# One core's hybrid decoder layer: queries and keys of both head pairs ahead of the other projections, the second norm's roots after the fourth product of the MLP, and MLP operands of two tile groups made during the output projection

## The chip, the cores and the metric

The kernel runs on one core of one Trainium2 chip. The metric is the device time of one execution in microseconds (us), as the median of several runs. An execution of this kernel runs five engines side by side: TensorE (PE, with its weight loads shown as PEld), VectorE (DVE), ScalarE (ACT), GpSimd (POOL), and SyncE (SP), which issues the loads and stores. Each engine takes its instructions in the order in which the program lists them, and waits at one until its operands and its target are free. So the order of the list on each engine is the schedule.

## The reference

One decoder layer over 1024 tokens of width 1024; the MLP's inner width is 4096. All data are float32.

```
u = rms_norm(x, norm1_g)
z = u @ w_in                       # 3584 columns
cb, cc, ch = split(z[:, :1536]);  rq, rk, rv, rg = split(z[:, 1536:], 4)
y_conv = group_rms_norm(cb * causal_dwconv3(cc * ch, conv_w), conv_norm_g, 8)
q = rotary(rq);  k = rotary(rk) * 128**-0.5          # 4 heads of 128
o = chunkwise_retention(q, k, rv)                    # chunks of 128 tokens
#   per chunk: o = (q k^T * decay) v + (q * xi) S;   S = gamma^128 S + (k * zeta)^T v
y_ret = group_rms_norm(o, ret_norm_g, 4) * silu(rg)
x = x + concat([y_conv, y_ret]) @ w_out
u = rms_norm(x, norm2_g)
x = x + (relu(u @ w_up) ** 2) @ w_down
out = rms_norm(x, final_norm_g)
```

## The kernel before

**Data.** Activations lie transposed: a tile is 128 features by 1024 tokens, cut in two halves of 512 tokens (`hs`). Every float32 operand is split into a high and a low part (`uh` and `ul`, `wh` and `wl`, the two halves of a `U` tile), and one product is three matmuls: high by high, high by low, low by high. ACT writes the high part, DVE or POOL subtracts to get the low part. `prepare` does this for the weight pieces some products ahead, from a planned list (`plan`, `parts`).

**Stages.** First come the values `v` of the retention heads and the token sums of the first norm (`rtok`, one root per token). Then the columns of `w_in`, 128 at a time, in the order of `IN_FIRST`: `rot_tiles` makes a rotated query or key of two heads from two column tiles (numbers 12 to 19), and `whole` makes a conv or gate tile (numbers 0 to 7). `tile_in` runs one column tile in four quarters, each with 12 matmuls of 128x512, into two PSUM banks. The remaining columns go by pairs (`pair_in`) and are computed by seven products in place of eight on combined operands, which `rights` prepares. Then comes `w_out` (`group`, four groups of eight steps, each step 12 matmuls), and then the MLP's up and down projections in blocks of seven products (`product`, `down_product`). The first block of the MLP is written by hand as a list, `rest`, with one entry for each of its 14 products (7 products for 2 tile pairs, `EARLY`). `at` counts them from 0.

**Rotary.** The first column tile's evacuation is four DVE multiplications into `ac` and `as`. The second's is eight DVE and four POOL operations, which give `q` (and the same for `k`).

**The first norm.** `spread_norms` copies the roots along a row (a DVE copy to a `t` tile) and multiplies by the identity matrix (`spread`, L304, 16 matmuls in all), so that ACT can write the root of each token to all partitions (`R`, `R2`). Conv and gate tiles are scaled by `R`; q and k are not, since the retention applies the norm per chunk. In the kernel before, it stands between q and k of pair 0.

**Retention.** `retention(p, q, k)` is a generator with one step for each of eight chunks and two more to drain. A step issues the scores of a chunk (L542, L547), the products of the chunk before (L571 to L579), and the transposes of the one before that (L609). DVE masks the scores to `h` and updates the state `S`; ACT and DVE make the output's root `m`, and ACT writes the normalized `h`.

**What sets the order.** A small planner runs while the program is written. It keeps a modelled clock per engine (`clock`, `now`). Work that isn't written in line is a task (`Task`, `spawn`), and `tick`, called after each quarter of a tile or each product, lets the tasks that are due issue their next instructions. A task yields the name of a mark that it waits for (`yield "retention", 1`). What has been issued is final. `force` runs a task up to a mark.

**The second norm.** `out_evac` adds each `w_out` result to the residual `x2` and collects squares in `sums_`. `token_rnorms` (L286) adds these over the partitions by 16 matmuls with one column each, takes root and reciprocal and copies them along rows; `spread` makes `r_half`. The MLP block's `take` adds products up; a finished block of 128x512 goes through `put`, which applies `max(c, 0) * r` and a square. The residual tiles that aren't needed for a while are written to DRAM (`put_aside`, pool `kept`) and read back (`fetch_back`).

**MLP operands.** `U` holds them by name: `11`, `21`, `22` are scaled quarters of the tiles, `t1` to `t4` sums of them; `put_hi` or `put_scaled_hi` is ACT's part, `put_lo` or `put_scaled_lo` DVE's. `group_todo(j)` lists those that are made during `w_out`, by step counted from the group's start; the others are made in `rest`. `new_basis` changes the residual tiles to the basis of the down products, on POOL.

All ACT, DVE and POOL operations are recorded through one helper, so their line in the profile is L65. L365 is the matmul of `mm`, L1173 that of the down products, L323 that of the values. These are the lines that a sentence can't say as well:

```
IN_WHOLE = [[0, 1, 2], [3, 4, 5, 6, 7]]
IN_FIRST = [12, 13, 16, 17] + IN_WHOLE[0] + [14, 15, 18, 19] + IN_WHOLE[1]
MLP_ORDER = (1, 2, 6, 5, 3, 7, 4)
EARLY = 2
```

## Time and profile before

| | us |
|---|---|
| median of 3 runs | 1115.47 (1114.19 to 1116.75) |
| profiled execution, own time | 1113.53 |
| its span | 1111.7 |
| PE busy | 1064.8, 96% of the span |
| DVE busy | 872.1, 78% |
| ACT busy | 462.1, 42% |
| POOL busy | 542.7, 49% |
| mean granted clock of TensorE | 0.985 of full speed |

The span is what the profiler saw of the program; the execution's own time is 1.83 us longer. Busy time is the sum over an engine's instructions. Matmuls are pipelined, so that a matmul's duration is longer than the distance to the next one. In the lists of instructions, a name is the program's with its number left out: `b` is a PSUM bank, `t` a temporary tile, `r` a raw weight piece or a row of roots.

### The profile page before, as it was taken

What the parts mean: (1) busy time and instruction counts of PE and PEld (TensorE: products, weight loads), DVE (VectorE), ACT (ScalarE), POOL (GpSimd) and SP (SyncE); (2) the same over time, 40 slices, a digit from 0 to 9 for tenths busy, and PEclk for the clock granted to TensorE, in tenths of its full rate; (3) what the DMA queues carried; (4) which work ended last, traced back from release to release, by engine and by line L of the source; (5) the groups of instructions that cost most, each with busy time, mean ns of one, the idle gap of its engine ahead of it and who ended that gap; (6) DMA issues with size and microseconds to landing.
All of it is one profiled execution on the core that took longest, in us unless ns stands there. A gap on an engine that the chain in (4) does not pass through costs nothing.

```text
span 1111.7 us, 13918 instructions
## 1 busy us (share of the span) xinstructions
PE 1064.8 (96%) x4916; PEld 885.2 (80%) x4916; DVE 872.1 (78%) x1207; ACT 462.1 (42%) x909; POOL 542.7 (49%) x377
## 2 busy tenths in 40 slices
PE   7979999999998699979999999999999999999997
PEld 6858888887777588868888888888888888888886
DVE  8441547548999745579999989989989899899945
ACT  8211461367336434344344333433343343434453
POOL 6130323414667323535827629538257276284553
PEclk9989999999999899989999999999999999999998
DMA  7111101240121523022130130121211211200204
GB/s 266 60 57 29 39 29 48 86 142 10 39 57 48 198 80 121 8 88 84 48 89 26 49 94 29 55 69 38 76 39 53 90 28 49 85 20 19 67 10 152
DMA packets 38294, 74.40 MB, mean 67 GB/s; under 512 B 4305, under 2 KB 6481, under 8 KB 38225
## 3 DMA queue, kind: packets, MB, share of 16 engines
q1 hardware_dynamic: 38224, 73.51, 21.0%
q8 instruction: 39, 0.64, 0.2%
q14 instruction: 31, 0.25, 0.1%
HBM read 67.73 MB, written 5.77 MB: 66 GB/s over the span
## 4 chain that ended last, share of the span: by engine, by line
PE 75%; DVE 12%; issue 2%; ACT 2%; POOL 1%; DVEq 0%; POOLq 0%; ACTq 0%
PE b L365 49%; PE b L1173 22%; DVE wl L65 2%; DVE z L65 2%; DVE r L65 1%; DVE U L65 1%; DVE x L65 1%; DVE t L65 1%; PE b L571 1%; PE b L542 1%; PE b L573 1%; PE b L579 1%; DVE xs L65 1%; DVE cv L65 1%; PE b L304 1%
## 5 line engine op out<-in xcount | busy, mean ns | idle before, releaser
L65 ACT CAST wh<-r 128x512 fp32r<-128x512 f32 x286 | 177.0, 621 | 375.4 <-PE b L365 195.7
L65 DVE TENSOR_TENSOR wl<-r,wh 128x512 fp32r<-128x512 f32 x249 | 227.5, 916 | 112.2 <-ACT wh L65 111.4
L365 PE MATMUL b<-U,wh 128*128 128x512 f32 x992 | 308.6, 392 | 7.1 <-DVE t L65 4.2
L65 POOL TENSOR_TENSOR r<-r,r 128x512 f32<-128x512 f32 x136 | 207.9, 1531 | 131.2 <-DVE wl L65 79.5
L1173 PE MATMUL b<-V,wh 128*128 128x512 f32 x784 | 241.9, 389 | 0.4 <-POOL V L65 0.4
L365 PEld LDWEIGHTS b<-U,wh 128*128 128x128 f32 x992 | 187.3, 189 | 47.8 <-issue 5.8
L65 DVE TENSOR_TENSOR x<-x,b 128x512 f32<-128x512 f32 (+1 forms) x320 | 197.9, 663 | 29.9 <-PE b L365 29.9
L365 PE MATMUL b<-U,wl 128*128 128x512 f32 x496 | 194.0, 391 | 0.0
L1173 PEld LDWEIGHTS b<-V,wh 128*128 128x128 f32 x784 | 147.1, 188 | 31.7 <-POOL V L65 0.8
L65 POOL TENSOR_TENSOR t<-t,t 128x512 f32<-128x512 f32 x70 | 106.7, 1529 | 102.6 <-ACT t L65 56.6
L1173 PE MATMUL b<-V,wl 128*128 128x512 f32 x392 | 152.5, 389 | 0.0
L65 POOL TENSOR_TENSOR wl<-r,wh 128x512 fp32r<-128x512 f32 x37 | 49.8, 1350 | 166.4 <-ACT wh L65 150.3
L365 PEld LDWEIGHTS b<-U,wl 128*128 128x128 f32 x496 | 93.8, 189 | 19.8
L365 PE MATMUL b<-uh,wh 128*128 128x512 f32 x320 | 106.5, 398 | 2.3 <-DVE z L65 2.3
L365 PE MATMUL b<-ul,wh 128*128 128x512 f32 x320 | 104.9, 393 | 1.6 <-DVE ul L65 1.5
L365 PE MATMUL b<-uh,wl 128*128 128x512 f32 x320 | 104.4, 391 | 0.0
L1173 PEld LDWEIGHTS b<-V,wl 128*128 128x128 f32 x392 | 73.6, 188 | 15.3
L65 POOL TENSOR_TENSOR V<-t,V 128x512 fp32r<-128x512 f32 x35 | 49.1, 1404 | 67.2 <-ACT V L65 67.2
L65 DVE TENSOR_TENSOR t<-t,b 128x512 f32<-128x512 f32 x112 | 75.8, 677 | 1.7 <-POOL t L65 1.2
L65 ACT ACTIVATE t<-t 128x512 f32<-128x512 f32 x64 | 40.3, 631 | 79.4 <-DVE t L65 78.7
L365 PEld LDWEIGHTS b<-ul,wh 128*128 128x128 f32 x320 | 60.3, 189 | 15.7 <-DVE ul L65 2.9
L365 PEld LDWEIGHTS b<-uh,wl 128*128 128x128 f32 x320 | 60.3, 189 | 12.9
(153 smaller groups left out, 1442.7 us busy)
## 6 DMA issues: line engine op xcount, KB each, us to landing
r<-w_up_t SPq DMA_DIRECT2D x64, 256.0 KB, 2.6
r<-w_down_t SPq DMA_DIRECT2D x56, 256.0 KB, 2.6
r<-w_in_t SPq DMA_DIRECT2D x48, 256.0 KB, 2.6
xt<-xT SPq DMA_DIRECT2D x16, 256.0 KB, 5.4
xs<-xT SPq DMA_DIRECT2D x8, 512.0 KB, 6.1
r<-w_out_t SPq DMA_DIRECT2D x16, 256.0 KB, 2.6
x<-xT SPq DMA_DIRECT2D x8, 512.0 KB, 7.9
outT<-out SPq DMA_DIRECT2D x6, 512.0 KB, 2.9
```

What stands on the lines that cost most here:

```text
L65: return f(out, *args, **kw)
L304: nc.tensor.matmul(b[:, c * P : (c + 1) * P], d, ident, start=True, stop=True)
L365: nc.tensor.matmul(b, a[:, k, :], rhs(n, k)[r], start=(start and i == 0), stop=(stop and i == len(ops) - 1),)
L542: nc.tensor.matmul(bs[:, js[j]], k[j][:, sl], q[j][:, sl], start=True, stop=True)
L571: nc.tensor.matmul(bo[:, js[j]], sc[:, js[j]], vj[j], start=True, stop=(S is None))
L573: nc.tensor.matmul(bo[:, js[j]], q[j][:, psl], S[:, js[j]], start=False, stop=True)
L579: nc.tensor.matmul(bk[:, js[j]], kz[:, js[j]], vj[j], start=True, stop=True)
L1173: nc.tensor.matmul(b, a, r, start=(i == 0), stop=(i == len(ops) - 1))
```

## The change

It has three parts.

1. `IN_FIRST` and the main loop take the query and key tiles of both head pairs first and the whole tiles after them. `spread_norms` is cut in two: `norm_rows` copies the roots along one row of 128x1024 after pair 0's queries, and the matmuls and ACT's writes follow after pair 1's keys. `retention(0)` therefore runs while pair 1's rotary tiles are computed and `retention(1)` while the first whole tiles are. Each has its own task entry, and the second waits for the end of the first.
2. `token_rnorms` is cut in `token_roots` (matmuls, root) and `rnorms` (reciprocal, row copies). In the MLP's first block the matmuls go from after the second product (`at == 1`) to after the fourth, the reciprocals to after the sixth, and `spread` from after the fourth product to after the ninth. Results are taken at once; a `put` that comes before the roots is kept in `waiting`.
3. For the tile groups 0 and 1 the operands `t3`, `t2`, `22` and `t4` are all made during `w_out`, and two more residual tiles are put aside, so that `rest` only has those of groups 2 and 3.

The diff:

```diff
 IN_PAIRS = [(8, 9), (10, 11), (20, 21), (22, 23)]
-IN_FIRST = [12, 13, 16, 17] + IN_WHOLE[0] + [14, 15, 18, 19] + IN_WHOLE[1]
+IN_FIRST = [12, 13, 16, 17, 14, 15, 18, 19] + IN_WHOLE[0] + IN_WHOLE[1]
 SLOT, LOOK, PE_MARGIN, LATE = 2.57, 2.0, 1.2, 0.0
...
 
-    def token_rnorms(sums_, r, pool_=None):
+    def token_roots(sums_, r, pool_=None):
 
...
         act.activation(r, b[:, :n], AF.Sqrt, bias=eps, scale=1.0 / D)
+        return r
+
+    def rnorms(r):
+
+        n = r.shape[-1]
         dve.reciprocal(r, r)
...
 
+    def token_rnorms(sums_, r, pool_=None):
+        return rnorms(token_roots(sums_, r, pool_))
+
     def spread(wide, pool_=None):
...
 
-    def spread_norms():
+    def norm_rows():
+        d = unit(s="d").rearrange("p (a b) -> p a b", b=P)
+        dve.tensor_copy(d, rtok[:, :, None].to_broadcast([P, NC_, P]))
+        return d
+
+    def spread_norms(d):
 
         for half, sl in enumerate(hs):
-            r = rtok[:, 4 * half : 4 * half + 4]
-            d = tmp().rearrange("p (a b) -> p a b", b=P)
-            dve.tensor_copy(d, r[:, :, None].to_broadcast([P, 4, P]))
-            b = spread([d[:, j] for j in range(4)])
+            b = spread([d[:, 4 * half + j] for j in range(4)])
             act.copy(R[:, sl], b)
...
 
-    o_n, retention_task = {}, [None]
+    o_n, retention_task = {}, [None, None]
 
...
         js = [slice(j * P, (j + 1) * P) for j in range(2)]
+        if p:
+            yield "retention", 0
         for c in range(NC_ + 2):
...
                         mark(("o", h0 + j, pc // 4), act)
-            retention_task[0].ready = max(clock[act], clock[dve])
+            retention_task[p].ready = max(clock[act], clock[dve])
             if c == NC_:
...
         if p == 0:
-            spread_norms()
+            rows_ = norm_rows()
         k = rot_tiles(*ropes)
...
         spawn(retention(p, q, k), max(clock[dve], clock[pool]))
-        retention_task[0] = procs[-1]
+        retention_task[p] = procs[-1]
         del q, k
-        if p == 0:
-            for f in IN_WHOLE[0]:
-                whole(f)
+    spread_norms(rows_)
+    for f in IN_WHOLE[0]:
+        whole(f)
 
...
     ct = ctx.enter_context(tc.tile_pool(name="ct", bufs=11))
-    kept = ctx.enter_context(tc.tile_pool(name="kept", bufs=3, space=bass.MemoryType.DRAM))
+    kept = ctx.enter_context(tc.tile_pool(name="kept", bufs=5, space=bass.MemoryType.DRAM))
     rv = ctx.enter_context(tc.tile_pool(name="rv", bufs=8))
...
 
-        t1 = lambda: un[j][:, lo_]
-        t3 = lambda: un[j][:, hi_]
-        return {
+        hi_of = lambda *names: [lambda x=x: put_hi(x, j, source(x, j)) for x in names]
+        lo_of = lambda *names: [lambda x=x: put_lo(x, j, source(x, j)) for x in names]
+        todo = {
             2: [lambda: put_scaled_hi("11", j, j, 0)],
...
             5: [lambda: put_scaled_lo("21", j, 4 + j, 0)],
-            8: [lambda: sum1(j), lambda: put_hi("t1", j, t1())],
-            9: [lambda: put_lo("t1", j, t1()), lambda: sum3(j)],
-            10: [lambda: sum2(j)] + [lambda: put_hi("t3", j, t3())] * (j < 3),
-            11: [lambda: put_lo("t3", j, t3())] * (j < 3),
+            8: [lambda: sum1(j)] + hi_of("t1"),
+            9: lo_of("t1") + [lambda: sum3(j)],
+            10: [lambda: sum2(j)],
         }
+        if j < 2:
+            todo[10] += hi_of("t3")
+            todo[11] = lo_of("t3") + hi_of("t2")
+            todo[12] = lo_of("t2") + [lambda: put_scaled_hi("22", j, 4 + j, 1)]
+            todo[13] = [lambda: put_scaled_lo("22", j, 4 + j, 1), lambda: sum4(j)] + hi_of("t4")
+            todo[14] = lo_of("t4")
+            todo[15] = [lambda: put_aside(4 + j)]
+        return todo
 
...
     todo[24] += [lambda: put_aside(2)]
-    todo[30] = [lambda: put_hi("t2", 0, source("t2", 0)), lambda: put_hi("t2", 1, source("t2", 1))]
+    todo[30] = [lambda: put_hi("t2", 2, source("t2", 2)), lambda: put_scaled_hi("22", 2, 6, 1)]
     for j in range(4):
...
 
-    r_half = [None, None]
+    r_half, waiting = [None, None], []
 
...
         def put(self, name, c):
-            self.c[name] = c
             r = r_half[int(name[1]) - 1]
+            if r is None:
+                waiting.append(lambda: self.put(name, c))
+                return
+            self.c[name] = c
             dve.scalar_tensor_tensor(c, c, 0.0, r, ALU.max, ALU.mult)
...
     rest = [
-        todo[32] + lo("t2", dve, 0, 1) + hi("t2", 2) + call(hi22, 0, 1),
-        todo[33] + lo("t2", dve, 2) + todo[34] + hi("t2", 3) + call(lo22, 0, 1) + call(hi22, 2, 3),
-        lo("t2", dve, 3) + hi("t3", 3) + call(lo22, 2, 3),
-        call(sum4, 0, 1) + hi("t4", 0, 1) + lo("t3", dve, 3),
-        call(sum4, 2, 3) + hi("t4", 2, 3) + call(fetch_back, 0, 1, 2),
-        lo("t4", dve, 0, 1),
+        todo[32] + lo("t2", dve, 2) + hi("t3", 2),
+        todo[33] + call(lo22, 2) + todo[34] + call(hi22, 3) + hi("t2", 3),
+        call(sum4, 2) + lo("t2", dve, 3) + hi("t3", 3) + lo("t3", dve, 2),
+        call(sum4, 3) + call(lo22, 3) + hi("t4", 2, 3) + call(fetch_back, 0, 1),
+        lo("t3", dve, 3) + call(fetch_back, 2, 4, 5),
         lo("t4", dve, 2),
         lo("t4", dve, 3),
-        call(new_basis, 5),
         call(new_basis, 7),
+        call(new_basis, 5),
         call(new_basis, 3),
         [],
+        [],
         [lambda: v_split(early, 1, 0)],
...
         b = early[p].product(n)
-        if at == 1:
-            wides = [token_rnorms([sums_[h]], rtok[:, 4 * h : 4 * h + 4]) for h in range(2)]
+        if at == 0:
             up.fetch(4)
-        if at == 3:
-            r_half[:] = [spread(w, pn) for w in wides]
         prepare()
...
         put_now()
-        if at == 2:
-            b2 = b
-            continue
-        if at == 3:
-            early[0].take(n, b2)
         early[p].take(n, b)
+        if at == 3:
+            roots = [token_roots([sums_[h]], rtok[:, 4 * h : 4 * h + 4]) for h in range(2)]
+        if at == 5:
+            wides = [rnorms(r) for r in roots]
+        if at == 8:
+            r_half[:] = [spread(w, pn) for w in wides]
+        while r_half[0] is not None and waiting:
+            waiting.pop(0)()
 
```

The order of the instructions shows it at three places. In these rows the first number is the place in the engine's list, then come the line, the operation, output and inputs with their numbers, the shape, and how many of it follow each other.

On PE, between pair 0's queries and its keys, before. The first two rows end the queries' second tile (weights `wl_531`), the last two begin the keys' first tile (`wh_564`):

```order
286 L365 MATMUL b_604<-ul_157,wh_530 128x512
287 L365 MATMUL b_605<-ul_157,wh_530 128x512
288 L365 MATMUL b_604<-uh_149,wl_531 128x512
289 L365 MATMUL b_605<-uh_149,wl_531 128x512
290 L304 MATMUL b_684<-ident,t_682 128x128 x4
291 L304 MATMUL b_693<-ident,t_691 128x128 x4
292 L365 MATMUL b_702<-uh_142,wh_564 128x512
293 L365 MATMUL b_703<-uh_142,wh_564 128x512
```

The same place after:

```order
286 L375 MATMUL b_604<-ul_157,wh_530 128x512
287 L375 MATMUL b_605<-ul_157,wh_530 128x512
288 L375 MATMUL b_604<-uh_149,wl_531 128x512
289 L375 MATMUL b_605<-uh_149,wl_531 128x512
290 L375 MATMUL b_686<-uh_142,wh_564 128x512
291 L375 MATMUL b_687<-uh_142,wh_564 128x512
292 L375 MATMUL b_686<-ul_150,wh_564 128x512
```

The spread's matmuls have left this place. After the change they stand on PE between pair 1's keys (weights `wl_1106`) and the first whole tile (`wh_1190`), with the row tile `d_682`:

```order
648 L375 MATMUL b_1314<-ul_157,wh_1105 128x512
649 L375 MATMUL b_1315<-ul_157,wh_1105 128x512
650 L375 MATMUL b_1314<-uh_149,wl_1106 128x512
651 L375 MATMUL b_1315<-uh_149,wl_1106 128x512
652 L312 MATMUL b_1399<-ident,d_682 128x128 x4
653 L312 MATMUL b_1406<-ident,d_682 128x128 x4
654 L375 MATMUL b_1413<-uh_142,wh_1190 128x512
655 L375 MATMUL b_1414<-uh_142,wh_1190 128x512
```

So some 360 rows of PE's list lie between the queries' end and the spread. On DVE, the evacuation of pair 1's second query tile (banks `b_1417`, `b_1418`) before:

```order
128 L65 TENSOR_TENSOR wl_1477<-r_1362,wh_1476 128x512
129 L65 TENSOR_TENSOR t_1480<-b_1417,rope_277 128x512
130 L65 TENSOR_TENSOR t_1481<-b_1417,rope_276 128x512
131 L65 TENSOR_TENSOR q_1416<-ac_1332,t_1480 64x512
132 L65 TENSOR_TENSOR q_1415<-t_1481,as_1333 64x512
133 L65 TENSOR_TENSOR t_1488<-b_1418,rope_277 128x512
134 L65 TENSOR_TENSOR t_1489<-b_1418,rope_276 128x512
135 L65 TENSOR_TENSOR q_1416<-ac_1332,t_1488 64x512
136 L65 TENSOR_TENSOR q_1415<-t_1489,as_1333 64x512
137 L65 TENSOR_TENSOR wl_1527<-r_1405,wh_1526 128x512
138 L65 TENSOR_TENSOR ac_1496<-b_1498,rope_276 128x512
```

and after (banks `b_942`, `b_943`; `bk` and `causal` mark the retention's masks, `S` its state, `m` its roots):

```order
98 L65 TENSOR_TENSOR t_1109<-b_942,rope_277 128x512
99 L65 TENSOR_TENSOR t_1110<-b_942,rope_276 128x512
100 L65 TENSOR_TENSOR q_941<-ac_834,t_1109 64x512
101 L65 TENSOR_TENSOR q_940<-t_1110,as_835 64x512
102 L65 TENSOR_TENSOR t_1117<-b_943,rope_277 128x512
103 L65 TENSOR_TENSOR t_1118<-b_943,rope_276 128x512
104 L65 TENSOR_TENSOR q_941<-ac_834,t_1117 64x512
105 L65 TENSOR_TENSOR q_940<-t_1118,as_835 64x512
106 L65 SCALAR_TENSOR_TENSOR h_1130<-b_1125,bk,causal 128x128 x2
107 L65 SCALAR_TENSOR_TENSOR S_1143<-S_1074,b_1136 128x128 x2
108 L65 SCALAR_TENSOR_TENSOR m_1147<-m_1147,bq 128x2
109 L65 RECIPROCAL m_1147<-m_1147 128x2
```

The same eight operations now have operations of pair 0's retention ahead of them and behind them, and before the change they had none.

On DVE, in the first products of the MLP's first block (`U` are operands; `un` holds their sums; `sm` the norm's weights; `wl` low parts of weights), before:

```order
377 L65 TENSOR_TENSOR U_3771<-un_3623,U_3771 128x512
378 L65 SCALAR_TENSOR_TENSOR un_3623<-x_3066,sm,un_3623 128x512
379 L65 TENSOR_TENSOR U_3775<-un_3459,U_3775 128x512
380 L65 SCALAR_TENSOR_TENSOR un_3623<-x_3066,sm,un_3623 128x512
381 L65 SCALAR_TENSOR_TENSOR U_3777<-x_3063,sm,U_3777 128x512
382 L65 SCALAR_TENSOR_TENSOR U_3779<-x_3064,sm,U_3779 128x512
383 L65 TENSOR_TENSOR wl_3856<-r_3317,wh_3855 128x512
384 L65 TENSOR_TENSOR U_3832<-un_3623,U_3832 128x512
385 L65 SCALAR_TENSOR_TENSOR U_3836<-x_3065,sm,U_3836 128x512
386 L65 SCALAR_TENSOR_TENSOR U_3838<-x_3066,sm,U_3838 128x512
387 L65 TENSOR_TENSOR wl_3889<-r_3489,wh_3888 128x512
388 L65 SCALAR_TENSOR_TENSOR un_3132<-x_3063,sm,un_3132 128x512
```

and after:

```order
376 L65 TENSOR_TENSOR un_3645<-un_3645 128x512
377 L65 TENSOR_TENSOR U_3743<-un_3469,U_3743 128x512
378 L65 TENSOR_TENSOR wl_3819<-r_3495,wh_3818 128x512
379 L65 TENSOR_TENSOR U_3798<-un_3645,U_3798 128x512
380 L65 SCALAR_TENSOR_TENSOR un_3645<-x_3064,sm,un_3645 128x512
381 L65 SCALAR_TENSOR_TENSOR U_3745<-x_3063,sm,U_3745 128x512
382 L65 SCALAR_TENSOR_TENSOR un_3645<-x_3064,sm,un_3645 128x512
383 L65 TENSOR_TENSOR wl_3848<-r_3315,wh_3847 128x512
384 L65 SCALAR_TENSOR_TENSOR un_3469<-x_3063,sm,un_3469 128x512
385 L65 TENSOR_TENSOR U_3830<-un_3645,U_3830 128x512
386 L65 TENSOR_TENSOR U_3801<-un_3469,U_3801 128x512
387 L65 TENSOR_TENSOR t_3857<-t_3803,b_3834 128x512
```

Before, this piece makes the operands `22` of four groups (`U_3777`, `U_3779`, `U_3836`, `U_3838`); after, the one operand `22` in it is group 2's (`U_3745`), and the addition of a product (`t_3857`) stands at its end.

More of the change, by code (lines that the diff above doesn't have):

```diff
@@ L1059, in put @@
         def put(self, name, c):
+            r = r_half[int(name[1]) - 1]
+            if r is None:
+                waiting.append(lambda: self.put(name, c))
+                return
             self.c[name] = c
-            r = r_half[int(name[1]) - 1]
             dve.scalar_tensor_tensor(c, c, 0.0, r, ALU.max, ALU.mult)
@@ L1131, in hybrid_layer @@
     rest = [
-        todo[32] + lo("t2", dve, 0, 1) + hi("t2", 2) + call(hi22, 0, 1),
-        todo[33] + lo("t2", dve, 2) + todo[34] + hi("t2", 3) + call(lo22, 0, 1) + call(hi22, 2, 3),
-        lo("t2", dve, 3) + hi("t3", 3) + call(lo22, 2, 3),
-        call(sum4, 0, 1) + hi("t4", 0, 1) + lo("t3", dve, 3),
-        call(sum4, 2, 3) + hi("t4", 2, 3) + call(fetch_back, 0, 1, 2),
-        lo("t4", dve, 0, 1),
+        todo[32] + lo("t2", dve, 2) + hi("t3", 2),
[3 more added lines that the diff above has]
+        lo("t3", dve, 3) + call(fetch_back, 2, 4, 5),
         lo("t4", dve, 2),
         lo("t4", dve, 3),
+        call(new_basis, 7),
         call(new_basis, 5),
-        call(new_basis, 7),
         call(new_basis, 3),
+        [],
         [],
@@ L1157, in hybrid_layer @@
         put_now()
-        if at == 2:
-            b2 = b
-            continue
+        early[p].take(n, b)
         if at == 3:
-            early[0].take(n, b2)
-        early[p].take(n, b)
+            roots = [token_roots([sums_[h]], rtok[:, 4 * h : 4 * h + 4]) for h in range(2)]
[5 more added lines that the diff above has]
+            waiting.pop(0)()
     def down_product(n, h):
```

## The prediction

> **What bounds the kernel now.** The page's first part comes first, to see which engine has no slack.
>
> ```profile
> span 1111.7 us, 13918 instructions
> PE 1064.8 (96%) x4916; PEld 885.2 (80%) x4916; DVE 872.1 (78%) x1207; ACT 462.1 (42%) x909; POOL 542.7 (49%) x377
> ```
>
> TensorE is busy for 1064.8 of 1111.7 us. The change removes no matmul, so time can come only from the 47 us in which PE stands still and from matmuls at a low clock. The second view is therefore PE's table of waits (engine, line, waited for: us in all, times, longest):
>
> ```profile
> PE b L304 <- DVE t L65: 10.0, 2, 9.0
> PE b L365 <- ACT z L65: 6.1, 1, 6.1
> PE b L446 <- DVE s L65: 4.4, 3, 3.4
> PE b L365 <- DVE t L65: 4.2, 1, 4.2
> PE b L365 <- DVE U L65: 1.2, 1, 1.2
> PE b L286 <- POOL t L65: 0.9, 1, 0.9
> ```
>
> One wait of 9.0 us is the spread of the first norm (L304) for its row tile; 6.1 us is the first projection product of w_out; 4.2, 1.2 and 0.9 us lie in the MLP's head. Those are the places the diff touches. The windows show whether each is a single wait or a stretch paced by another engine (from:to, length, then busy us and counts of PE, PEld, DVE, ACT, POOL, granted clock, DMA share, GB/s):
>
> ```profile
> 277.84:375.91 98.07, 82.27 (x345) 64.69 (x344) 94.60 (x90) 43.17 (x71) 66.70 (x46) 0.98 0.18 52
> 400.00:465.60 65.60, 65.60 (x291) 54.34 (x290) 34.53 (x45) 26.01 (x44) 22.39 (x16) 1.00 0.26 80
> 465.64:517.80 52.16, 45.81 (x202) 37.61 (x201) 42.02 (x59) 24.01 (x43) 22.25 (x17) 0.93 0.29 92
> 517.80:1000.00 482.20, 481.92 (x2126) 398.43 (x2125) 451.90 (x626) 190.57 (x331) 285.73 (x190) 1.00 0.18 54
> ```
>
> In the first row (the projections by pairs, up to the first w_out product) DVE works 94.60 of 98.07 us and PE 82.27: DVE sets the pace. In the second (w_out) PE has no gap and DVE is idle 31 us. In the third (the MLP's head) both wait and the clock is 0.93. In the fourth PE never stops at 0.227 us a matmul (481.92/2126); its instructions stay as they are, so it keeps its length.
>
> **The change, part 1: q and k of both head pairs first, spread of the norm later.** Start us, length, engine, instruction, in brackets the idle time before:
>
> ```profile
> 75.31 1.29 DVE L65 TENSOR_TENSOR t<-b,rope 128x512 f32<-128x512 f32 x2 [7.39 <-PE b L365]
> 83.90 0.76 DVE L65 COPY t<-rtok 128x512 f32<-128x512 f32 x2
> 84.39 3.72 PE L304 MATMUL b<-ident,t 128*128 128x128 f32 x16 [8.96 <-DVE t L65]
> 87.82 0.73 PE L365 MATMUL b<-uh,wh 128*128 128x512 f32 x2
> 481.05 1.95 PE L304 MATMUL b<-ident,t 128*128 128x128 f32 x16
> 482.75 0.71 PE L365 MATMUL b<-U,wh 128*128 128x512 f32 x2
> ```
>
> The spread matmuls stand in PE's queue right behind q's second tile, and their operand behind that tile's rotary evacuation on DVE, which lasts from 75.31 to 83.90 (8.59 us). PE idles 8.96 us, and the 16 small matmuls then take 3.43 us (84.39 to 87.82) where the same 16 take 1.70 in the second norm (481.05 to 482.75). After the change k's first tile stands there instead, whose banks and weights are free, and the copy of the norm's rows is made one whole tile before its matmuls, so the wait goes with nothing late behind it: 8.96 + 1.73 = 10.7 us.
>
> The new order brings a new wait. Retention of pair 0 now runs between pair 1's rotary tiles. At each quarter of a tile PE issues one retention step, whose scores DVE must mask. In DVE's new order the evacuation of pair 1's second q tile stands between two such steps.
>
> ```profile
> 122.77 0.71 PE L365 MATMUL b<-uh,wh 128*128 128x512 f32 x2
> 125.61 0.60 PE L542 MATMUL b<-q,q 128*128 128x128 f32 x4
> 127.75 0.71 PE L365 MATMUL b<-uh,wh 128*128 128x512 f32 x2
> 126.47 0.61 DVE L65 SCALAR_TENSOR_TENSOR h<-b,bk,causal 128x128 f32<-128x128 f32 x2 [1.70 <-PE b L547]
> 129.68 0.62 ACT L65 ACTIVATE h<-b,m 128x128 f32<-128x128 f32 x2 [0.23 <-DVE m L65]
> ```
>
> From the end of that q tile PE has a retention step (125.61 to 127.75, 2.14 us), two quarters (2.84 each, 122.77 to 125.61) and the next scores (0.60) ahead of the product that needs the masked scores: 8.4 us. DVE gives them after 8.59 + 0.61 = 9.2 us, 0.8 late. The chain behind them, from mask to normalized output (126.47 to 130.30, 3.8 us), is late for the transposes one step on by about as much again. I take 1.7 us; the bounds are 0 and 8.6 (a full evacuation bare). The first tile's evacuation of each rotary pair is four such operations, some 2.6 us (4 x 0.645), less than a quarter. Part 1: -10.7 + 1.7 = **-9.0**.
>
> Retention of pair 1 then runs between the first whole tiles instead of the later ones, so the four later `rights` (w_in's combined weights, which from the second on wait for that retention) and a group norm start about 40 us earlier. This relieves DVE where it sets the pace:
>
> ```profile
> 277.84 0.39 PE L365 MATMUL b<-uh,wh 128*128 128x512 f32 x1
> 281.23 1.21 DVE L65 TENSOR_TENSOR a<-a,b 128x512 f32<-128x512 f32 x2
> 375.09 0.68 DVE L65 TENSOR_TENSOR z<-z,b 128x512 f32<-128x512 f32 x1
> 375.91 0.76 PE L365 MATMUL b<-yh,wh 128*128 128x512 f32 x1 [6.06 <-ACT z L65]
> L65 DVE RECIPROCAL r<-r 128x512 f32<-128x512 f32 x6 | 20.1, 3342 | 1.3 <-ACT r L65 1.3
> L65 DVE SCALAR_TENSOR_TENSOR z<-z,sm,r 128x512 f32<-128x512 f32 x6 | 6.7, 1117 | 0.1
> L65 DVE TENSOR_TENSOR z<-z,cv 128x512 f32<-128x512 f32 x4 | 4.8, 1196 | 0.1
> L65 DVE TENSOR_TENSOR s<-t,s 128x512 fp32r<-128x512 f32 x1 | 1.7, 1743 | 0.0
> ```
>
> The last four rows group this stretch's operations (busy us, mean ns). At 277.84 PE has done the last whole tile and DVE first evacuates it at 281.23, 3.39 us behind, with a reciprocal of 3.34 just ahead. The end is DVE's too: the first w_out product waits for a bank which the operation at 375.09 frees (375.77, PE at 375.91), though the table names ACT. In the new order that reciprocal and its partner lie ahead of the tile's last quarters, and I let the 3.39 go. From the tile's evacuation to the last combination DVE has 87 operations before and 88 after: one reciprocal less (3.34), two z,sm,r less (2.2), two z,cv less (2.4), against two s more (3.5) and small additions (about 2.3), -2.1 by these means. Sum **-5.5**. If DVE's backlog returns it is 0; if PE becomes the pace it is 82.27 - 98.07 = -15.8. I stay near the first, since 88 operations remain where 87 were.
>
> **Parts 2 and 3: roots later; operands of two tile groups early.** The sums of the second norm wait 0.93 us for POOL. PE then computes one product (12 matmuls) at half speed. Later it waits 1.23 us for an operand and 4.19 us for a bank, and has another slow product:
>
> ```profile
> 472.95 1.29 PE L286 MATMUL b<-ones,t 128*128 128x1 f32 x8 [0.93 <-POOL t L65]
> 474.11 1.20 PE L365 MATMUL b<-U,wh 128*128 128x512 f32 x2
> 478.31 0.62 PE L365 MATMUL b<-U,wh 128*128 128x512 f32 x2
> 494.17 1.19 PE L365 MATMUL b<-U,wh 128*128 128x512 f32 x2 [4.19 <-DVE t L65]
> 498.57 0.62 PE L365 MATMUL b<-U,wh 128*128 128x512 f32 x2
> 455.56 0.69 DVE L65 TENSOR_TENSOR U<-un,U 128x512 fp32r<-128x512 f32 x1
> 458.16 1.70 DVE L65 TENSOR_TENSOR wl<-r,wh 128x512 fp32r<-128x512 f32 x1 [1.25 <-ACT wh L65]
> 458.03 1.28 POOL L65 TENSOR_TENSOR r<-r,r 128x512 f32<-128x512 f32 x1
> ```
>
> A product at full speed is 12 x 0.227 = 2.72 us; the slow ones take 4.20 (474.11 to 478.31) and 4.40 (494.17 to 498.57), 3.16 us more together. With the gaps (0.93 + 1.23 + 4.19 = 6.35) 9.5 us can be won. DVE is busy 42.0 of 52.2 us here. Eight of its operand operations leave (low parts of t2, 22 and t4 and a sum, for two groups) and one comes, -7 of 0.69 to 1.70 us, 5 to 12 us of its work. They go into w_out, where DVE's 31 idle us cover them; were those full, the w_out products would wait for the same 5 to 12 us. The sums now stand three products in, when the squares are long made; takes no longer wait for the roots, so banks come free earlier. Instead the two finished blocks `11` wait in tmp tiles, off PSUM, until the spread at the ninth product; they are next read when V is split at the 13th, four products (some 11 us) on, so that costs nothing while DVE is less than that behind. The fetch of the next up block moves one product earlier in SP's queue, ahead of the fetches back: nothing, as its data are first read behind this block. By DVE's new order it stays some 3 us behind PE by the seventh product and the low part of the last group's t2 arrives about when it is needed; for that I leave 1.5 us. **-8.0**, bounds -10.5 and 0. Two more x2 tiles are stored to memory and fetched back for the down products; DMA is at 0.26 to 0.29 in these rows and the need is behind all of the first block: nothing, covered by that block. If they came late, the down products would wait for them.
>
> One rule speaks against part 3. The Trainium skill ("SBUF — State Buffer", section "Who interferes with whom") says that a DVE instruction with two SBUF inputs contends with a GpSimd instruction that reads SBUF and that the loser blocks. This trace agrees: the same subtraction takes 0.69 us at 455.56 and 1.70 us beside POOL's operation of 458.03. By that rule the eight moved operations, beside a POOL busy 22.39 of 65.60 us, would get about 8 x 0.34 x 1.0 = 2.7 us longer (an estimate), which w_out's 31 idle us cover; the sum stands by either.
>
> A second one touches the roots: "TensorE: Matmul & The Clock Gate", section "What's actually happening", in the Trainium skill, halves the clock after an idle window of about 3.4 us. Here the slow product at 474.11 followed a gap of only 0.93 and 16 one-column matmuls, so those may count as idle; if they do again, the head keeps 1.5 us and the time is 1094.5.
>
> **Sum.** -9.0 - 5.5 - 8.0 = -22.5 against the span of 1111.7: 1089.2. The profiled execution's own time was 1113.53, 1.83 around its span; the median of the runs is 1115.47, 1.94 above that. So 1091.0 for such an execution and **1093.0** for the median.
>
> **Rivals.** (a) Only the norm's wait goes; DVE keeps the pace in the pair stretch and in the head, whose gaps reappear under other names. For it: the 94.60 of 98.07, and seven operations are less than a tenth of DVE's instructions in the two stretches. Against: 4.2 of the head's wait hangs on deferred takes, which go. 1115.5 - 9 - 2 = 1104 (1098 to 1109).
>
> (b) Relief of DVE counts for more, since operations that ran beside POOL get shorter too; the pair stretch falls near PE's own 82.3. Another 8 to 10 us: 1083. Against: POOL has 40 operations there where it had 44, hardly less.
>
> (c) The other side: retention between rotary evacuations exposes each evacuation bare, as the spread was. Two second tiles at 8.6, two first tiles at 2.6 and 1.7 of slow clock behind each of the three longer pauses make 27 us; less the 24 won it is 1118.5, slower. It decides from the point where PE comes to the masked scores right behind the evacuation and not 8.4 us later; the new order has two quarters of matmuls between.
>
> (d) PE's waits move unchanged into the new places, 1115.5: every term would have to fail at once.
>
> **How the numbers follow.** The forecast (1085 to 1100) has 0.65, (a) 0.20, (b) 0.09, (c) 0.03, (d) 0.03. A measurement of this kernel can tell some 0.2%, 2.2 us. Faster is the forecast, (a) and (b), less 0.01 for (a)'s upper end: 0.93; (d) is 0.03 for the same; (c) and that 0.01 make 0.04 slower. The range reaches down to (b)'s middle and up to (a)'s: 1084 to 1104; outside lie half of (a), half of (b) and the last two, 0.2.
>
> **What would show it.** Right: no wait over 1 us of the spread; the stretch up to w_out's first product shorter by about 5; no wait of a head product for a DVE t or U over 1 us, and the clock near 1.00 there. A wait of the retention for DVE's h or S of about 1.7 us shows the new price. Wrong: retention waits of 5 us and more beside pair 1's tiles (c), w_out's first product still waiting 6 us with a stretch of 98 (a), a slow product behind the roots, or down products that wait for a DMA.

## The result, and the profile after

The changed kernel takes 1098.97 us (median of 4 runs, 1098.7 to 1099.68) against 1115.84 for the kernel before in the same runs: a ratio of 0.985 (95% interval 0.983 to 0.987), 16.9 us less. The forecast was 22.5 less. Its profiled execution took 1098.8 us with a span of 1097.0, 14.7 under the span before. The two differences are not the same because the profiled execution before was 1.94 us under its kernel's median and the one after 0.17. The head of the page:

```profile
span 1097.0 us, 13933 instructions
PE 1064.2 (97%) x4916; PEld 885.6 (81%) x4916; DVE 874.1 (80%) x1206; ACT 461.6 (42%) x909; POOL 544.7 (50%) x377
```

PE's busy time is the same as before, so the time came out of its pauses. PE's table of waits after (line numbers have moved: L375 was L365, L312 was L304, L455 and L456 were L445 and L446, L583 was L571):

```profile
PE b L375 <- DVE z L65: 9.0, 3, 5.1
PE b L331 <- DVE vh L65: 5.3, 1, 5.3
PE b L455 <- ACT s L65: 4.0, 1, 4.0
PE b L375 <- DVE U L65: 2.9, 1, 2.9
PE b L583 <- ACT h L65: 1.8, 1, 1.8
PE b L312 <- DVE t L65: 1.0, 1, 1.0
```

The 9.0 us wait of the first norm's spread is gone; the 1.0 left at L312 is in the final norm and was there before. New are 4.0 us at L455, the sums of a group norm (before, such sums waited 0.34 and 0.60 in this part of the execution, and 0.92 and 3.42 in the pair stretch), 2.9 for a `U` of the MLP's head, and 1.8 for the retention's `h`. The windows of the pair stretch, w_out, the head up to the first down product, and the MLP from the head's last product on, with the columns as before:

```profile
274.13:366.49 92.36, 83.02 (x345) 66.23 (x344) 89.06 (x90) 42.45 (x70) 59.88 (x40) 0.95 0.19 55
366.49:455.58 89.09, 89.09 (x384) 73.62 (x385) 51.22 (x71) 39.65 (x67) 25.13 (x19) 0.98 0.39 139
455.58:506.16 50.58, 47.63 (x213) 39.36 (x212) 39.89 (x57) 22.50 (x40) 24.69 (x19) 0.93 0.27 94
503.44:990.00 486.56, 486.55 (x2147) 402.52 (x2146) 455.01 (x629) 192.82 (x334) 289.17 (x193) 1.00 0.18 54
```

DVE's work in the pair stretch fell from 94.60 to 89.06 us, and the stretch by as much, from 98.07 to 92.36. The head kept a clock of 0.93.

Every kernel below runs the same 3120 matmuls of `mm`, so the starts of the same numbered matmul divide each execution into the same stages: all before the first pair product, the pair stretch, w_out, the head (up to the first down product), and the rest (up to the last matmul's end). Lengths in us from the profiled executions, with the median of the timed runs:

| kernel | up to pairs | pairs | w_out | head | rest | median | ratio to before, 95% interval |
|---|---|---|---|---|---|---|---|
| before | 277.84 | 98.07 | 89.73 | 54.72 | 585.07 | 1115.47 | |
| changed | 274.13 | 92.36 | 89.09 | 50.58 | 584.41 | 1098.97 | 0.985 (0.983 to 0.987) |
| part 1 alone | 274.89 | 92.31 | 89.12 | 53.16 | 587.07 | 1104.89 | 0.992 (0.990 to 0.993) |
| spread later alone | 267.51 | 99.06 | 88.83 | 53.17 | 587.06 | 1103.46 | 0.990 (0.989 to 0.992) |
| part 2 alone | 279.06 | 98.17 | 89.72 | 53.11 | 585.41 | 1113.91 | 1.000 (0.999 to 1.001) |
| part 3 alone | 278.10 | 98.14 | 89.93 | 49.13 | 585.58 | 1108.77 | 0.995 (0.993 to 0.997) |
| t2 early | 274.87 | 92.30 | 89.15 | 46.82 | 584.68 | 1096.76 | 0.985 (0.983 to 0.986) |
| norm's sums late | 268.38 | 92.75 | 88.85 | 50.43 | 584.44 | 1093.18 | 0.981 (0.980 to 0.983) |
| rights late | 268.69 | 108.86 | 88.95 | 50.47 | 584.43 | 1108.79 | 0.995 (0.993 to 0.996) |
| both reorderings | 268.63 | 92.78 | 89.09 | 46.85 | 586.19 | 1091.02 | 0.979 (0.978 to 0.981) |
| both, without part 2 | 268.66 | 92.76 | 89.15 | 50.06 | 584.72 | 1092.90 | 0.980 (0.979 to 0.982) |
| old order, all else | 267.77 | 98.16 | 89.93 | 46.80 | 585.06 | 1095.76 | 0.983 (0.981 to 0.984) |

One of the four runs of "norm's sums late" took 2765.12 us, for a reason that no trace shows, and is left out (with it the median is 1093.66). Where the code of a stage is the same, the stages repeat within 1.2 us, the head of the kernel before within 1.6 (the last section shows why) and the rest within 2.7. Where the rest is longer, PE has short waits in it that the changed kernel lacks: with both reorderings 0.74 us for a `t` of ACT at 533.83; in part 1 alone 0.68 for a `V` at 511.23 and 0.75 for that `t` at 546.86. By stage the change gives -3.71, -5.71, -0.64, -4.14 and -0.66: -14.9.

### The profile page after: what moved, and what is told of

The parts are those of the page before. It is cut to its first block, busy times and chain, and to the rows that moved or that the text cites. A ratio compares the mean times of both kernels' runs of the same rounds, so it can differ in the third digit from the quotient of the medians.

```text
span 1097.0 us, 13933 instructions
## 1 busy us (share of the span) xinstructions
PE 1064.2 (97%) x4916; PEld 885.6 (81%) x4916; DVE 874.1 (80%) x1206; ACT 461.6 (42%) x909; POOL 544.7 (50%) x377
## 4 chain that ended last, share of the span: by engine, by line
PE 84%; DVE 10%; ACT 3%; issue 2%; POOL 1%; DMA 0%; SPq 0%; DVEq 0%; POOLq 0%; ACTq 0%
PE b L375 54%; PE b L1195 24%; PE b L331 2%; DVE wl L65 2%; DVE U L65 1%; DVE z L65 1%; ACT uh L65 1%; ACT t L65 1%; DVE cv L65 1%; DVE r L65 1%; DVE t L65 1%; PE b L583 1%; PE b L554 1%; DVE q L65 1%; PE b L312 1%
## 5 line engine op out<-in xcount | busy, mean ns | idle before, releaser
L65 DVE TENSOR_TENSOR wl<-r,wh 128x512 fp32r<-128x512 f32 x253 | 230.0, 912 | 106.5 <-ACT wh L65 105.8
L375 PE MATMUL b<-U,wh 128*128 128x512 f32 x992 | 308.1, 392 | 2.9 <-DVE U L65 2.9
L375 PEld LDWEIGHTS b<-U,wh 128*128 128x128 f32 x992 | 187.5, 189 | 42.6 <-DVE U L65 3.4
L375 PE MATMUL b<-U,wl 128*128 128x512 f32 x496 | 194.2, 392 | 0.0
L65 POOL TENSOR_TENSOR wl<-r,wh 128x512 fp32r<-128x512 f32 x33 | 44.2, 1341 | 150.7 <-ACT wh L65 126.2
L375 PE MATMUL b<-uh,wh 128*128 128x512 f32 x320 | 107.7, 401 | 4.0 <-DVE z L65 4.0
L375 PEld LDWEIGHTS b<-U,wl 128*128 128x128 f32 x496 | 93.8, 189 | 19.5
L375 PE MATMUL b<-ul,wh 128*128 128x512 f32 x320 | 106.0, 396 | 0.0
L375 PE MATMUL b<-uh,wl 128*128 128x512 f32 x320 | 105.6, 395 | 0.0
L375 PEld LDWEIGHTS b<-uh,wh 128*128 128x128 f32 x320 | 59.8, 192 | 16.4 <-issue 2.7
L375 PEld LDWEIGHTS b<-uh,wl 128*128 128x128 f32 x320 | 61.2, 191 | 13.3
L375 PEld LDWEIGHTS b<-ul,wh 128*128 128x128 f32 x320 | 60.9, 190 | 13.1
```

What stands on the lines that cost most here:

```text
L65: return f(out, *args, **kw)
L375: nc.tensor.matmul(b, a[:, k, :], rhs(n, k)[r], start=(start and i == 0), stop=(stop and i == len(ops) - 1),)
```

## The experiments

**The parts alone.** The first kernel has only part 1 of the diff.

> Part 1 alone (queries and keys of both pairs first, spread after them), parts 2 and 3 left as before. By the two traces part 1 is worth 9.4 us of the change's 14.8: 12.7 at the first norm's spread, less 9.0 given back among the whole tiles, and 5.7 in the pair stretch. Theory: a time of 1106 (1105 to 1107.5), the 4.0 us wait of PE for the group norm's s among the whole tiles present, the head of the MLP as before with its waits of 4.2, 1.2 and 0.9 us. Rival: part of that 9.4 needs the shorter head (nothing in the stages says so), then 1109 and more.

Measured: 1104.89, 9.9 less than the 1114.80 of the kernel before beside it, with 4.03 us of waiting at the group norm's sums. The time is 0.1 us under the expected range, and by stages the agreement is less good: its head was 1.6 us shorter and its rest 2.0 longer than before, with the same code there. The head's waits were not the 4.2, 1.2 and 0.9 us of before, but 2.65, 2.87 and 0.94, which is about the same sum.

The second keeps the old order and moves only the spread (`spread_norms` is cut in two as in the change):

```diff
         if p == 0:
-            spread_norms()
+            rows_ = norm_rows()
         k = rot_tiles(*ropes)
+        if p == 0:
+            spread_norms(rows_)
...
```

> The old order of all projections; only the spread of the first norm moved one rotary tile pair later, behind pair 0's keys, its row copy made where the spread stood. Theory: this alone takes the whole wait: 8.96 us and 1.73 of slow clock, so 1105 (1104 to 1106.5), as good as the whole reorder; pair stretch still 98 us with a first w_out wait of 6. Rival 1: the spread behind the keys waits for something else, 1109 to 1115. Rival 2: the time won is handed back in the pair stretch, where DVE sets the pace, because DVE's work there waits for nothing earlier: 1108 to 1112.

Measured: 1103.46, 11.3 less, 0.5 under the expected range. The spread's new place takes the wait alone, and the reorder of queries and keys on top was worth nothing in this form: its 6.8 us in the pair stretch (99.06 to 92.31) pay for 7.4 lost up to the pairs (267.51 to 274.89). Rival 1 falls, since PE has no wait left at the spread (the 1.0 us at L304 is in the final norm); rival 2 falls, since the stretch stays within 1 us of the 98.07.

The third has only part 2, the fourth only part 3.

> Part 2 alone (roots, reciprocals and spread of the second norm later, takes at once), with all operands still made in the head. Theory: the bank wait of 4.2 us came from takes put off until the roots were spread, so it goes with its slow product of 1.7, and the 0.9 wait with 1.5; but DVE still has seven operations more than in the changed kernel, so a wait for an operand grows to some 4 us with slow clock behind it: head 2 us shorter, 1113.5 (1111.5 to 1115.5). Rival: roots were all of it, head 4 us or more shorter as in the changed kernel, 1111.5 or less.

> Part 3 alone (operands of tile groups 0 and 1 made during w_out, two more tiles put aside), roots and spread at their old places. Theory: the wait for the roots and the deferred takes stay, so that the 0.9 and the 4.2 us waits stay about as they are, the 1.2 us wait for U goes: head 1 to 2 us shorter, 1114 (1112.5 to 1115.5). Rival: the operands were what kept DVE late, the 4.2 wait goes too: head 4 us shorter or more, 1111.5 or less. In both w_out keeps its 65.6 us.

Measured: part 2 gives 0.9 us (its interval holds no change), part 3 gives 6.0, with a head 5.6 us shorter where 1 to 2 were expected. The three parts alone add up to 16.8 us, about what the change gives. Part 3's theory is wrong: with fewer operands on DVE the wait for the bank fell from 4.2 to 0.8 us although the take was still put off. In the waits of part 3 alone:

```profile
PE b L286 <- POOL t L65: 0.9, 1, 0.9
PE b L365 <- DVE t L65: 0.8, 1, 0.8
PE b L365 <- DVE U L65: 0.7, 1, 0.7
```

And in those of part 2 alone:

```profile
PE b L373 <- DVE U L65: 3.0, 1, 3.0
PE b L373 <- ACT U L65: 1.6, 2, 1.3
```

Here the wait for POOL at the roots' sums is gone, and a `U` makes PE wait in its place. The head of part 2 alone, 53.11 us, is no shorter than that of part 1 alone (53.16) and of the spread alone (53.17), whose heads have the code of before. So with all operands on DVE in the head, the operands and not the roots set when it could go on; the rival of part 3 holds and that of part 2 falls. The 0.8 us is not the operands' work alone: with the same takes and the same set of operands, but no slow product ahead of it, the wait for the bank is 2.63 us in the version without part 2 below.

**The head: which operand.** In the changed kernel PE stops within the fifth product, after ten of its twelve matmuls, so that it waits for the low part of the fourth group's `t2`. On DVE that operation stands at 471.88, behind a weight piece that waited 1.69 us for ACT and behind a sum of another operand. It is the first of the two in the last row and took 1.75 us, beside an operation of POOL (471.38 to 473.08); the second took 0.68:

```profile
470.60 0.69 DVE L65 TENSOR_TENSOR wl<-r,wh 128x512 fp32r<-128x512 f32 x1 [1.69 <-ACT wh L65]
471.21 0.75 DVE L65 SCALAR_TENSOR_TENSOR un<-x,sm,un 128x512 f32<-128x512 f32 x1
471.88 2.35 DVE L65 TENSOR_TENSOR U<-un,U 128x512 fp32r<-128x512 f32 x2
```

What the wait costs besides its 2.95 us is in the window behind it, where the clock is 0.50 and 14 matmuls take 6.13 us in place of 3.18, 2.95 more:

```profile
468.16:473.69 5.53, 2.58 (x13) 1.78 (x12) 3.84 (x6) 3.28 (x6) 1.70 (x1) 0.94 0.01 1
473.69:479.82 6.13, 6.13 (x14) 4.77 (x15) 5.49 (x7) 2.94 (x6) 4.31 (x3) 0.50 0.37 126
```

The experiment changes the order within `rest`:

```diff
-        todo[33] + call(lo22, 2) + todo[34] + call(hi22, 3) + hi("t2", 3),
-        call(sum4, 2) + lo("t2", dve, 3) + hi("t3", 3) + lo("t3", dve, 2),
+        todo[33] + todo[34] + hi("t2", 3) + call(lo22, 2) + lo("t2", dve, 3) + call(hi22, 3),
+        call(sum4, 2) + hi("t3", 3) + lo("t3", dve, 2),
```

> The changed kernel, only the order within two entries of the MLP's head list changed: the last group's sum for t2, its high part and its low part go ahead of the low part of 22 of group 2, the high part of 22 of group 3 and one sum. Nothing is added or removed. Theory: PE's wait of 2.95 us for U in the fifth product is for exactly this low part, and the slow clock of 3.3 us is behind that gap, not behind the 16 one-column matmuls; both go: head 6 us shorter, 1093 (1092 to 1095). Rival 1: the one-column matmuls by themselves halve the clock for one product, 1094.5. Rival 2: DVE sets the pace of the head, and the wait comes back at a later operand or bank: 1096 to 1099.

Measured: the wait is gone and the head is 46.82 us in place of 50.58, 3.8 less and not 6. The time is 1096.76, in the range of rival 2 and 2.2 less than the changed kernel's; the two were timed beside different runs of the kernel before (1114.04 and 1115.84), and their ratios overlap (0.985 and 0.985), so the gain of this edit alone rests on its stage and on the comparison with both reorderings below. The windows of its head, from the product behind the roots' sums on:

```profile
468.90:471.76 2.86, 2.86 (x14) 2.34 (x14) 1.91 (x4) 2.75 (x6) 0.00 (x0) 1.00 0.01 3
471.76:475.09 3.33, 2.89 (x14) 2.10 (x12) 3.33 (x5) 1.15 (x3) 1.74 (x1) 1.00 0.04 6
475.09:478.65 3.56, 2.98 (x13) 2.17 (x13) 3.41 (x4) 2.38 (x5) 3.03 (x2) 1.00 0.26 73
478.65:482.19 3.54, 2.98 (x12) 2.17 (x13) 3.06 (x4) 2.10 (x4) 1.65 (x2) 1.00 0.94 339
```

The clock is 1.00 throughout, so the one-column matmuls alone, which take 1.70 us with no wait among them, did not slow it, and rival 1 falls. But three products now take 3.3 to 3.6 us in place of 2.72, with waits of 0.44, 0.56 and 0.58 us among them for a bank, a weight piece and a root: rival 2 in part, 2.3 us of the 6.

**The group norm's sums.** In the changed kernel, among the whole tiles:

```profile
252.80 0.61 PE L375 MATMUL b<-uh,wl 128*128 128x512 f32 x2
257.44 0.49 PE L455 MATMUL b<-s,blkr 128*128 128x512 f32 x1 [4.03 <-ACT s L65]
258.76 1.05 PE L375 MATMUL b<-uh,wh 128*128 128x512 f32 x2
261.32 0.69 PE L375 MATMUL b<-uh,wh 128*128 128x512 f32 x2
```

In the kernel before, the same sums' first two matmuls:

```profile
272.65 0.40 PE L445 MATMUL b<-s,blkr 128*128 128x512 f32 x1
273.39 0.50 PE L446 MATMUL b<-s,blkr 128*128 128x512 f32 x1 [0.34 <-DVE s L65]
```

Their place in PE's list moved: before, 756 matmuls of `mm` stand ahead of them, and after, 708, one whole tile fewer. The planner puts them where its own clock says that they are ready. Two matmuls of the second convolution tile's norm wait in PE's queue, and the next six run at half speed (258.76 to 261.32, 2.56 us where six others take 1.36). DVE just before, with two operations of POOL and two of ACT:

```profile
247.99 1.28 DVE L65 TENSOR_TENSOR U<-xs,U 128x512 fp32r<-128x512 f32 x2
249.20 1.52 DVE L65 SCALAR_TENSOR_TENSOR cv<-a,sm,cv 128x511 f32<-128x511 f32 x2
250.46 1.41 POOL L65 TENSOR_TENSOR wl<-r,wh 128x512 fp32r<-128x512 f32 x1 [3.54 <-ACT wh L65]
250.64 1.78 DVE L65 TENSOR_TENSOR U<-xs,U 128x512 fp32r<-128x512 f32 x1
252.34 1.53 DVE L65 SCALAR_TENSOR_TENSOR cv<-a,sm,cv 128x512 f32<-128x512 f32 x2
253.98 1.29 DVE L65 TENSOR_TENSOR z<-b,R 128x512 f32<-128x512 f32 x2
254.81 1.26 POOL L65 TENSOR_TENSOR z<-z,cv 128x512 f32<-128x512 f32 x1 [2.94 <-DVE z L65]
256.11 0.63 ACT L65 ACTIVATE t<-z 128x512 f32<-128x512 f32 x1 [5.73 <-POOL z L65]
256.77 0.62 ACT L65 CAST s<-t 128x512 fp32r<-128x512 f32 x1
```

The operations `U<-xs,U` are those of the `rights`, which now start here; the tile `z` whose squares the norm sums comes behind them, and POOL's product and ACT's square and high part `s` follow it. Two experiments, one that gives the sums' matmuls a later place (a larger margin for this one task, two quarters further on in PE's list, behind 732 matmuls of `mm`; the lines that hand the margin on are left out) and one that starts the `rights` later:

```diff
-                    if task.ready + PE_MARGIN <= now[0] or look > 1e6:
+                    if task.ready + task.margin <= now[0] or look > 1e6:
...
-        asked.append((o, blkr, 1.0 / 64, done, clock[eng], LATE * half))
+        asked.append((o, blkr, 1.0 / 64, done, clock[eng], LATE * half, 8.0 if i == 1 else PE_MARGIN))
```

> The changed kernel, only the sums of the second convolution tile's group norm (the matmuls that waited 4.03 us for s among the whole tiles) put two quarters later in PE's list. Theory: PE's 4.03 and the 1.2 us of slow clock behind them go, DVE still makes the reciprocals ahead of the last whole tile's evacuation, so the pair stretch stays: 5 us less, 1094 (1093 to 1096). Rival: DVE is the bound from there to the end of the pairs, and what PE gains it loses again in the pair stretch, which grows from 92.4 to 97 us: 1098 to 1100.

```diff
         if j:
-            yield "retention", 1
+            yield "y", 1, 0
```

> The changed kernel, but the later three rights (combined operands of w_in's pairs) wait until the second convolution tile's norm is done, not only for the second retention. Theory: their operations on DVE are what made s late, so that the wait of 4.03 us for s and the slow clock behind it go (5 us); but they then run in the pair stretch, which DVE paces, and it grows from 92.4 back to 97 or 98 us: about no change, 1099 (1097 to 1101). Rival 1: s was late for another reason, the wait of 4 us stays: 1103 or more. Rival 2: the pair stretch has room and keeps its length: 1094.

Measured for the later sums: 1093.18 us, the stage up to the pairs 5.8 shorter, the pair stretch 92.75 (92.36). The theory holds and the rival falls: PE's pause bought DVE nothing. Measured for the later rights: the wait at the sums is gone too (268.69), with the sums still behind 708 matmuls, which shows that the rights' work made `s` late for that place. But the time is 1108.79. That lies in the range of rival 1, whose reason (the wait stays) is not what happened, and neither theory nor rival foresaw where it went:

```profile
PE b L375 <- ACT uh L65: 12.8, 1, 12.8
PE b L375 <- DVE z L65: 8.5, 2, 6.7
```

The program makes all four `t1` before it writes the pair products, and the third of these reads them: PE computes two products and then stands still for 12.85 us, up to 287.14. The rights have to be early for their own sake.

**Together, and what the parts are worth then.**

> The changed kernel with both reorderings, the norm's sums two quarters later and the last t2 earlier. Theory: they lie in different stages, the gains add: 1088 (1086.5 to 1091). Rival: each gain comes back as a wait in the stage behind it, 1093 or more.

Measured: 1091.02, the best version here, 8 us under the changed kernel and at the upper end of what was expected. Its four runs (1090.63 to 1091.77) lie below the three of the later sums (1093.08 to 1094.14), which were timed beside the same runs of the kernel before. Stages show both gains (268.63 and 46.85), with 1.8 us more in the rest, where the 0.74 us wait for ACT's `t` stands: the rival in part. The next two kernels take something away from it: the first has part 2 undone, the second the old order with the later spread and no change to the norm's sums.

> The version with both reorderings, but without part 2: roots, row copies and spread of the second norm stand again after the second and the fourth product, and the take of the third waits for them. Theory: part 2 alone was worth 0.9 us only because the operands kept DVE late; with these out of the way it shows its own value: the wait of 0.9 us for POOL, the bank wait behind the put-off take (0.8 to 2.7 us) and a slow product behind one of them come back: 1094 (1093 to 1096) against 1091. Rival: part 2 is worth nothing here either, since without it PE only stands elsewhere: 1090.5 to 1092.

> The old order of projections with the spread one tile pair later, together with parts 2 and 3 and the earlier t2: everything but the reorder of queries and keys. Theory: the spread alone gave as much as the whole part 1 (11.3 and 9.9 us), but its pair stretch stays at 99 us where the reordered kernel has 92.5; the reorder with the norm's sums later is therefore ahead by about 5: 1096 here (1095 to 1097.5) against 1091. Rival: the pair stretch wins nothing by the reorder once the head is fixed: 1091 to 1093.

Measured: 1092.90 without part 2, between theory and rival. Its head is 50.06 us where 46.85 stood, with waits of 0.95 us for POOL and 2.63 for a bank; but its rest is 1.5 shorter, without the wait for ACT's `t`, and the intervals of the ratios (0.979 to 0.982 and 0.978 to 0.981) overlap. That part 2 saves 3 us in the head is shown in one profile each; what it saves in all stays open between nothing and 3. The old order takes 1095.76, as expected, with a pair stretch of 98.16: the reorder is worth 4.7 us by the medians and 3.8 by the ratios (0.9825 and 0.9791) once the sums do not wait, as against nothing before.

## Why the prediction was right, and where it was off

Direction and range held: 1098.97 lies within 1085 to 1100. It also lies within the 1098 to 1109 of rival (a), so the time alone does not tell the two apart; the stages do, since the pair stretch fell by 5.71 us where (a) had it stay. By the medians a quarter of the forecast gain did not come, by the spans a third (14.7 came of 22.5): the 1.94 us that the forecast added for the median was 0.17 in the changed kernel, and that luck hid part of the miss. The miss comes from two terms.

- **The norm's spread, -10.7**: measured -12.65 at the first product of the keys, 1.7 of it given back by the 16 matmuls at their new place: about -11.0.
- **The retention's new wait, +1.7**: measured 1.80 at the products that need the masked scores, behind the evacuation that was named, and 0.20 at the transposes. The sum fits better than its parts: the forecast had 0.8 at the products and about as much again at the transposes. DVE's mask was 1.0 us late there, and an operation of ACT behind it, which the working lacked, made up the rest of the 1.80.
- **What the part's list lacked**: the sums of the group norm. I let the `rights` and the norm "start about 40 us earlier" as pure relief and did not follow what stands behind them on DVE, and where the norm's matmuls come to stand on PE, in the stage that receives them; the row `PE b L446 <- DVE s`, 4.4 us, stood in the table of waits, and no term used it. It cost 4.26 us of waiting and 1.2 of slow clock. Up to the quarter before these matmuls the changed kernel led by 8.52 us (it began that quarter at 250.53, the kernel before at 259.05), near the forecast; part 1 up to the pairs then gave -3.7 and not -9.0, and -9.5 once the sums stood later (268.38). This is the step that failed.
- **The pair stretch, -5.5**: measured -5.71, with DVE's work 5.54 less. The first w_out product still waits, 5.09 us for `z`, so DVE still sets the end there; the view that DVE paces the stretch held. Its two parts missed by about 1 us each, in opposite directions: DVE's first evacuation came 1.07 us behind the last whole tile (275.20 against 274.13) in place of 3.39, a gain of 2.3 and not 3.4, and its work from there to the operation that frees w_out's bank fell by 3.4 and not 2.1.
- **The head, -8.0**: measured -4.14. The place was right ("the low part of the last group's t2 arrives about when it is needed"), the 1.5 us left for it were not: PE waited 2.95, and the clock ran at half for 6.13 us behind it, 2.95 more. The slow clock that follows a wait was not in the 1.5, though the same profile showed it twice. Two of the signs that were to show the forecast right therefore did not come: no wait over 1 us for a `U`, and a clock near 1.00 in the head. A sign of a wrong one came, a slow product behind the roots, though the wait for the operand made it.
- **Which of parts 2 and 3**: I ascribed the 4.2 us bank wait to the takes that were put off. Part 3 alone removed most of it; part 2 alone left the head as long as it was and only renamed the waits.
- **What the moved operations and DMA might add to w_out**: nothing, as said; w_out took 89.09 where 89.73 were, with 71 operations of DVE for 64 and 4.3 us more of its work, and no down product waits for a load.

The rule of the Trainium skill on the ports ("SBUF — State Buffer", section "Who interferes with whom") bears on the result once more: one subtraction of the `rights` took 1.78 us at 250.64, beside POOL's operation of 250.46, and two took 1.28 together at 247.99. That agrees with the section's contention between GpSimd's reads and DVE's second input; no run here took POOL's part away.

## What to carry to other kernels

Work that is taken off a crowded stretch has to be followed into the stretch that receives it: not only "is there idle time", but which matmul in the in-order queue will then wait, and for how long. A wait that is long enough costs twice, since matmuls behind it can run at half speed: here 1.2 us more behind the 4.03 us wait at the norm's sums, and 2.95 more behind the 2.95 us wait in the head. Before a large reorder is made, try the smallest edit that removes the wait: here a move by one tile pair gave all of it, and the reorder paid only after a second norm's sums had been moved as well.

## What was not expected of the hardware

Nearly the same pause was followed by different clocks. The roots' 16 one-column matmuls go in two groups of eight, with a wait of 0.93 to 0.95 us between them when they stand at their old place. The next product had a granted clock of 0.65 in the kernel before and 0.62 in part 3 alone, but 1.00 in part 1 alone and in two others.

The granted clock in the traces shows why. From its first record, 9 to 12 us in, it changes only on a grid: every stretch at 0.50 lasts 3.41 us or two to four times that, except one that runs on to the end of each program, and within an execution all limits fit one grid of 3.41 us. Where the grid lies against the program differs from execution to execution. Here are the stretches of the grid around the pause in part 3 alone (471.61 to 474.43, one-column matmuls included), and then around that in part 1 alone (461.76 to 464.57):

```profile
470.98:474.39 3.41, 2.47 (x20) 2.27 (x19) 3.34 (x3) 0.40 (x2) 2.46 (x2) 1.00 0.00 0
474.39:477.81 3.42, 3.42 (x10) 2.74 (x10) 0.72 (x3) 3.39 (x8) 0.00 (x0) 0.50 0.01 2
477.81:481.22 3.41, 3.41 (x16) 2.83 (x16) 3.38 (x8) 0.70 (x2) 0.00 (x0) 1.00 0.00 0
```

```profile
460.13:463.55 3.42, 2.58 (x16) 2.18 (x15) 2.34 (x2) 1.05 (x2) 3.34 (x3) 1.00 0.00 0
463.55:466.96 3.41, 3.31 (x19) 2.90 (x20) 1.80 (x3) 2.78 (x5) 0.05 (x1) 1.00 0.01 2
466.96:470.37 3.41, 3.41 (x18) 2.86 (x17) 1.66 (x6) 2.28 (x5) 0.00 (x0) 1.00 0.00 0
```

In part 3 alone 2.78 us of the pause fall into one stretch, and the next runs at 0.50. In part 1 alone a limit of the grid cuts the pause into 1.78 and 1.02, and the clock stays. The twelve traces agree up to 1050 us, with no exception. Of the stretches at full clock without one-column matmuls, 44 have PE idle for 1.83 us or more, and behind each the next is at 0.50; 3508 have 1.81 or less, and behind each the next is at 1.00. For the roots' sums this comes out as well if the one-column matmuls count as idle, or nearly so, though the profile calls PE busy in them: the two kernels whose next product slowed have 2.53 and 2.78 us of waiting and one-column matmuls in one stretch, the ten others 1.88 at most. Without a wait these matmuls last only 1.70 us, which fits that they did not slow the clock in the experiment with the earlier t2. Longer waits can be cut too: one of 2.63 us in the version without part 2 lies in one stretch, and the product behind it took 4.41 us; one of 2.65 in part 1 alone is cut into 1.77 and 0.88, and its product took 2.82.

The Trainium skill ("TensorE: Matmul & The Clock Gate", section "What's actually happening") says that the window of activity is 3413 ns long and runs freely, so that it does not start with the kernel; the grid in these traces agrees with both. For the half clock it names an idle window, and here 1.83 us of idle time in 3.41 were enough. A stage with such a pause therefore has a length that is known only to some 1.6 us, and a single profile can't settle less.
